# Forgetting attention: key sums subtracted inside the maximum, sample rows divided at the result

## The chip, the core and the metric

The kernel runs on one core of one Trainium2 chip. The metric is the device time of one execution in microseconds (us); the time of a kernel is the median of its timed runs. The engines of the core are TensorE (PE; its weight loads have a row of their own, PEld), VectorE (DVE), ScalarE (ACT), GpSimd (POOL) and SyncE (SP), which here mostly starts transfers. Each engine takes its instructions in the order in which they stand in its queue.

## The reference

One inference step of an encoder layer: stick-breaking attention, a Mamba-2 SSD group and forgetting attention run side by side on the same normalised input; then come an output projection, cross-attention and a feed-forward block. What the change touches is the forgetting attention ("fox"):

```python
def fox_attend(q, k, v, fq, fk, q_pos, k_pos):
    s = jnp.einsum('bqhd,bkhd->bhqk', q, k).astype(jnp.float32) * (HEAD_DIM ** -0.5)
    s = s + (jnp.transpose(fq, (0, 2, 1))[..., :, None] - jnp.transpose(fk, (0, 2, 1))[..., None, :])
    valid = k_pos[None, :] <= q_pos[:, None]
    p = jax.nn.softmax(jnp.where(valid, s, -jnp.inf), axis=-1)
    return jnp.einsum('bhqk,bkhd->bqhd', p, v.astype(jnp.float32)).astype(q.dtype)
```

fq and fk are the same running sum of log forget gates (fcum = cumsum(logf)), taken at the query and at the key. For one query, fq is one number for all keys, so in exact arithmetic it drops out of the softmax.

There are 4 fox heads of 64 columns. The prompt is one stream of 1024 tokens. The samples are 8 streams of 16 new tokens, each with 1024 cached keys and values, so a sample row has 1024 + 16 keys; the kernel lays out 128 columns for the new keys of all streams and masks.

## The kernel before, in words

**Tiling.** A row of work is 128 queries against their keys. For the prompt there are 4 heads x 8 blocks of 128 queries; block qb has (qb + 1) x 128 keys, taken in pieces of 512. For the samples there are 4 groups (two streams x 4 heads x 16 queries = 128 rows) with 1152 columns: two pieces of 512 cached keys and one of 128 new ones.

**One prompt row** (`prompt_rows`, then `fox_rows`). The key sums of the head lie in a tile "xc", loaded once per head by `fcb_of` (L732) and spread over the 128 partitions. L532, on ScalarE, writes fq - fk into a tile "ws" over the whole width of the row. Then for each piece TensorE makes the scores in a PSUM tile "pss" (L562, L563, and the mask with L565), and L536, on VectorE, adds ws to them, writes the sum back to ws and takes the running maximum into a small tile "sm". L540 negates the maximum, L542 (ScalarE) takes the exponential and its sum, L543 the reciprocal, and L549 (VectorE; the constant FSC is "D" throughout) multiplies the row by it.

**Behind two rows** (`prompt_av`) TensorE transposes the weights (L580), ScalarE copies them out (L583, tile "pt"), TensorE multiplies by the values (L595, PSUM "pso"), ScalarE (L603, L606) and VectorE (L604) take the result, and SP stores it (L608).

**One group of sample rows** (`decode_units`). The cached keys come by DMA (L883, tile "wr"), are transposed on TensorE and copied by ScalarE (L891, tile "kf"); L874 makes the scores. The key sums of the cached keys come by L910 into a tile "xc" (from fs_sc), those of the new keys lie in "fnew", and the query's own sum in "fqs"; L532 has two passes per group, over 1024 and 128 columns. Then the row goes the same way as a prompt row. In `av` the weights are transposed and copied (L926, into the tile "act"), multiplied by the new and the cached values (L934; the values come by L943), and L953 (VectorE) multiplies the result by a head mask "maskh"; L960 stores it. The stick-breaking samples run through the same `av` with m == 0.

**What runs beside it.** `pipeline` hands out rows and their products, first of the stick-breaking attention (m == 0), then of the fox (m == 1), with the sample groups inserted after units 4, 8, 12 and 16 of the latter; between two steps `fill_all` puts in a piece of the dense input projections (L328 to L330) and, when these are done, of the SSD blocks. An SSD block loads its inputs with three transfers (L1038, L1040, L1042, into a tile "act"), transposes and copies them (L1055 to L1060), makes decay weights with ScalarE (L1078, L1083) and VectorE (L1097), and ends with a norm (L1162) and a store (L1171). SP also loads the residual rows (L1282, into "st" and "xc") towards the end of the stage.

**The order.** The program is recorded in the order in which these generators emit it; then a list scheduler with a timeline of its own reorders it, engine by engine, by priority and by estimated readiness:

```python
with tile.TileContext(nc, schedule_with_timeline_sim=True) as tc:
```

So an edit in `fox_rows` also changes where other instructions stand.

**Buffers.** "ws" has 7 buffers, "xc" 3, "act" 6, "pss" 2. A transfer into a buffer waits in SP's queue until its last reader is done, and everything behind it in that queue waits too. The key sums in "xc" are last read by L532.

Of the kernel before, what the change touches and what calls it, by code (L numbers as in the profile page):

```python
# [12 lines left out]
ALU = mybir.AluOpType  # L13
# [49 lines left out]
def tile_hybrid_step(ctx: ExitStack, tc: tile.TileContext, a: dict):  # L63
# [459 lines left out]
        pool_tt(sg[:, :n - 1], sg[:, :n - 1], kp[:, 1:n], ALU.mult)  # L523
        return sg

    fcount = [0]

    def fox_rows(n, pieces, fkb, fq):
        sp = ws_t()
        mx = small(6)  # L530
        for c0, w, fk in fkb:
            ACT.activation(sp[:, c0:c0 + w], fk, AF.Identity, bias=fq, scale=-1.0)  # L532
        for i, (c0, w, emit) in enumerate(pieces):
            ps = pS()
            emit(ps[:, :w])
            DVE.tensor_tensor_reduce(out=sp[:, c0:c0 + w], in0=ps[:, :w], in1=sp[:, c0:c0 + w],  # L536
                                     op0=ALU.add, op1=ALU.max, scale=1.0,
                                     scalar=-3e38 if i == 0 else mx[:, i - 1:i], accum_out=mx[:, i:i + 1])
        np_ = len(pieces)
        DVE.tensor_scalar(mx[:, 3:4], mx[:, np_ - 1:np_], -1.0, None, ALU.mult)  # L540
        s = sp[:, :n]
        ACT.activation(s, s, AF.Exp, bias=mx[:, 3:4], accum_out=mx[:, 4:5])  # L542
        DVE.reciprocal(mx[:, 5:6], mx[:, 4:5])  # L543
        fcount[0] += 1
        e = FSC[fcount[0] % len(FSC)]
        if e == "A":
            ACT.activation(s, s, AF.Copy, scale=mx[:, 5:6])
        else:
            (DVE if e == "D" else POOL).tensor_scalar(s, s, mx[:, 5:6], None, ALU.mult)  # L549
        return sp  # L550

    def prompt_rows(m, qs, kh, kl, qb, fcb=None, fq=None):
        n = (qb + 1) * P
        mask = mask_fx if m else mask_sb
        pieces = []
        for c0 in range(0, n, 512):
            w = min(512, n - c0)

            def emit(ps, c0=c0, w=w):
                q = qs[:, qb * P:(qb + 1) * P]  # L560
                last = c0 + w == n
                PE.matmul(ps, q, kh[:, c0:c0 + w], start=True, stop=False)  # L562
                PE.matmul(ps, q, kl[:, c0:c0 + w], start=False, stop=not last)  # L563
                if last:
                    PE.matmul(ps[:, w - P:w], identr, mask, start=False, stop=True)  # L565
            pieces.append((c0, w, emit))
        if m == 0:
            return sb_rows(n, pieces)
        return fox_rows(n, pieces, [(0, n, fcb[:, :n])], fq)

    def prompt_av(h, qp, w0, w1, vt, kt_row):

# [40 lines left out]
    def prompt_units(m, h, fcb_of=None):  # L613
        env = {}

        def load():
            if not env:
                env["st"] = load_stacks(m, h)
                env["fcb"] = fcb_of(h) if m else None

        def row(qb):
            load()
            qs, kh, kl, _ = env["st"]
            return prompt_rows(m, qs, kh, kl, qb, env["fcb"], fqc[:, qb, h:h + 1] if m else None)

        def unit(qp):
            return ([lambda: row(2 * qp), lambda: row(2 * qp + 1)],
                    lambda w: prompt_av(h, qp, w[0], w[1], env["st"][3], 2 * m + h // 2))
        return [unit(qp) for qp in (range(4) if (m, h) not in REV else range(3, -1, -1))], load
# [23 lines left out]
    fqc = mcst.tile([P, 8, 4], F32, name="fqc")  # L653
    fnew = mcst.tile([P, P], F32, name="fnew")
    fqs = mcst.tile([P, 4], F32, name="fqs")

    def fox_sums():
        l = log1p_exp_negabs(lf, [P, NBLK, 4])
# [182 lines left out]
    def decode_units(m):  # L841
# [15 lines left out]
        def rows(p):  # L857
# [49 lines left out]
            if m == 0:  # L907
# [1 line left out]
            fkb = xc_t()  # L909
            SP.dma_start(out=fkb[:, :PAST],  # L910
                         in_=fs4[8 * p:8 * p + 8].rearrange("r i k -> (r i) k").unsqueeze(1).to_broadcast([32, 4, PAST]))
            return fox_rows(T, pieces, [(0, PAST, fkb[:, :PAST]), (PAST, P, fnew)], fqs[:, p:p + 1]), hold

        def av(p, w, hold):
            vsm = new[1]

            wt = hold[:, P:P + 1024] if m else st_t(F32)
            wn = hold[:, P + 1024:2 * P + 1024] if m else sg2_t()[:, :P]
            for k0 in (0, 4, 8):
                nk = min(4, 9 - k0)  # L920
                tp = pT()
                for k in range(nk):
                    wk = w[:, 8 * P:9 * P] if k0 == 8 else \
                        w[:, k0 * P:(k0 + 4) * P].rearrange("q (p k) -> q p k", k=4)[:, :, k]
                    PE.transpose(tp[:, k * P:(k + 1) * P], wk, ident)
                ACT.copy(wn if k0 == 8 else wt[:, k0 * P:(k0 + 4) * P], tp[:, :nk * P])  # L926

            po = pO()

            def quads(w, moving, start, stop):  # L930
                def one(g):
                    v = moving(g // 2, g % 2)
                    out = po[32 * g:32 * g + 32, :P]
                    return PE.matmul(out if len(v.shape) == 2 else out.rearrange("p (h d) -> p h d", h=2),  # L934
                                     w[:, 32 * g:32 * g + 32], v, start=start, stop=stop)
                return [lambda g=g: one(g) for g in (3, 0, 1, 2)]

            work = quads(wn, lambda b2, nb: vsm[:, 2 * nb:2 * nb + 2, 0, :], True, False)
            for hf in range(2):
                raws = []  # L940
                for b2 in range(2):
                    raw = ring.tile([P, 1056], F32, tag=("wh", "wl")[b2], name="vr")
                    SP.dma_start(out=raw[:, :1024].rearrange("p (k c) -> p k c", c=256),  # L943
                                 in_=cv[2 * p + b2, hf * 512:(hf + 1) * 512, :]
                                 .rearrange("(p k) c -> p k c", k=4))
                    raws.append(raw)
                for k in range(4):
                    work += quads(wt[:, (4 * hf + k) * P:(4 * hf + k + 1) * P],
                                  lambda b2, nb, raws=raws, k=k: raws[b2][:, k * 256 + nb * P:k * 256 + (nb + 1) * P],
                                  False, hf == 1 and k == 3)  # L950
            together(work)
            ob = sg2_t()[:, :P]
            DVE.tensor_tensor(out=ob.rearrange("p (h d) -> p h d", h=2),  # L953
                              in0=po[:, :P].rearrange("p (h d) -> p h d", h=2),
                              in1=maskh.unsqueeze(2).to_broadcast([P, 2, 64]), op=ALU.mult)
            of = pT()
            PE.matmul(of[:, :64], ob, fold2.rearrange("p n t -> p (n t)"), start=True, stop=True)
            on = sg2_t()[:, :64]
            DVE.tensor_copy(on, of[:, :64])
            SP.dma_start(out=mix_sc[2 * m:2 * m + 2, :, SEQ + 32 * p:SEQ + 32 * p + 32].rearrange("n p t -> p n t"),  # L960
                         in_=on.rearrange("p (n t) -> p n t", n=2))
# [1105 lines left out]
```

## Time and profile before

| what | value |
|---|---|
| median of 3 runs | 1888.05 us (1887.65 to 1890.45) |
| profiled execution, its own time | 1882.73 us |
| span of the profile | 1881.0 us |
| mean granted TensorE clock | 0.993 |
| PE busy | 1821.7 us (97%) |
| PEld busy | 1628.8 us (87%) |
| DVE busy | 892.0 us (47%) |
| ACT busy | 822.5 us (44%) |
| POOL busy | 613.0 us (33%) |

The profile shows one execution. The span runs from its first to its last instruction; some 1.7 us of the execution's time lie around it. A row such as "L532 ACT ACTIVATE ws<-xc,fqs 128x1024 x4 | 4.6, 1156" gives the line, the engine, what is written and read, the count, then the busy time in us and the mean of one in ns; behind a second bar stands the idle time of the engine just before, and what ended it. In the list of waits "PE pss L874 <- DVE sm L536: 3.6, 2, 2.7" reads: TensorE was idle for 3.6 us before L874 and VectorE's L536 ended it, in 2 waits, the longest of 2.7. SPq is SP's queue of transfers. In the busy times by stretch each column is the busy time in that stretch, and the share "DMA" is of the core's 16 DMA engines. In the chain of waits a row gives its start, its length and the work.

### The profile page before, as it was taken

The numbers are of one execution on the slowest core, as the hardware profiler recorded it, in microseconds if no ns is written. First come the engines' busy times: TensorE is split into PE (matmuls) and PEld (weight loads), VectorE is DVE, ScalarE is ACT, GpSimd is POOL, SyncE is SP. The second block draws the span as 40 slices with busy tenths as digits, with TensorE's granted clock in tenths as the row PEclk, the third lists the DMA queues.
The fourth block names the chain that finished last, engine by engine and source line by source line (L and its number), as shares of the span: only waits on it lengthen the run. The fifth ranks groups of instructions, "written<-read, shape, count | busy, mean of one in ns | idle before, by whom it ended". The sixth has DMA issues, their size and how long they took to land.

```text
span 1881.0 us, 32406 instructions
## 1 busy us (share of the span) xinstructions
PE 1821.7 (97%) x12136; PEld 1628.8 (87%) x12136; DVE 892.0 (47%) x1802; ACT 822.5 (44%) x1751; POOL 613.0 (33%) x921
## 2 busy tenths in 40 slices
PE   7999989999998989999999989999999999999998
PEld 5899878888867768899988889999999999788886
DVE  3412333566667873444443596333333334455554
ACT  6532543545567862344432464333333333344433
POOL 7622424445116653101112107444444542000000
PEclk9999998999999999999999989999999999999999
DMA  9464754437688782245585124332222223657572
GB/s 336 151 191 149 217 146 124 149 111 202 209 240 267 269 276 95 107 137 178 173 284 188 68 73 123 79 83 72 71 71 71 71 72 104 216 185 239 178 245 88
DMA packets 291069, 296.64 MB, mean 158 GB/s; under 512 B 80092, under 2 KB 242884, under 8 KB 290912
## 3 DMA queue, kind: packets, MB, share of 16 engines
q1 hardware_dynamic: 290912, 294.57, 49.9%
q8 instruction: 96, 1.57, 0.3%
q14 instruction: 61, 0.50, 0.1%
HBM read 225.12 MB, written 69.91 MB: 157 GB/s over the span
## 4 chain that ended last, share of the span: by engine, by line
PE 62%; DMA 3%; DVE 2%; ACT 2%; issue 1%; POOL 1%; SPq 0%; DVEq 0%; POOLq 0%; ACTq 0%
PE psd L1869 11%; PE pst L1869 8%; PE psd L328 5%; PE psd L329 5%; PE psd L330 5%; PE pss L1869 4%; PE pss L328 3%; PE pss L329 3%; PE pss L330 3%; PE pso L1869 2%; PE pst L328 1%; PE pst L329 1%; PE pst L330 1%; PE pso L328 1%; PE pso L330 1%
## 5 line engine op out<-in xcount | busy, mean ns | idle before, releaser
L132 POOL TENSOR_TENSOR wl<-wr,wh 128x256 fp32r<-128x256 f32 (+2 forms) x184 | 138.4, 784 | 230.8 <-ACT wh L292 220.0
L328 PE MATMUL psd<-act,wh 128*128 128x384 f32 x528 | 181.4, 344 | 0.0
L329 PE MATMUL psd<-act,wh 128*128 128x384 f32 x528 | 180.7, 342 | 0.0
L330 PE MATMUL psd<-act,wl 128*128 128x384 f32 x528 | 180.7, 343 | 0.0
L1869 PE MATMUL pst<-bT,tr 128*128 128x256 f32 (+1 forms) x1068 | 155.0, 293 | 0.0
L1869 PEld LDWEIGHTS pst<-bT,tr 128*128 128x128 f32 x1068 | 144.9, 188 | 0.1
L330 PE MATMUL psd<-wh,act 128*128 128x512 f32 (+3 forms) x424 | 136.5, 323 | 0.0
L329 PE MATMUL psd<-wl,act 128*128 128x256 f32 (+3 forms) x414 | 133.9, 324 | 1.9 <-POOL wl L132 1.9
L328 PE MATMUL psd<-wh,act 128*128 128x256 f32 (+3 forms) x414 | 132.9, 325 | 1.0 <-DMA act<-osc 0.9
L1869 PE MATMUL psd<-bT,tr 128*128 128x320 f32 (+1 forms) x912 | 133.0, 295 | 0.4 <-POOL tr L132 0.4
L1869 PEld LDWEIGHTS psd<-bT,tr 128*128 128x128 f32 x912 | 125.1, 189 | 0.7 <-POOL tr L132 0.7
L132 POOL TENSOR_TENSOR tr<-u,tr 128x256 fp32r<-128x256 f32 x110 | 82.4, 778 | 102.3 <-ACT tr L1705 84.8
L253 POOL TENSOR_SCALAR sm<-sm 128x1 f32<-128x1 f32 (+2 forms) x27 | 7.0, 260 | 301.4 <-ACT y L1971 207.2
L1844 DVE TENSOR_TENSOR tr<-tr,pst 128x256 f32<-128x256 f32 (+1 forms) x86 | 38.6, 449 | 139.9 <-ACT tr L1841 106.7
L132 POOL TENSOR_TENSOR ws<-ws 128x256 f32<-128x256 f32 (+2 forms) x100 | 69.7, 724 | 99.1 <-DVE ws L522 90.8
L330 PEld LDWEIGHTS psd<-act,wl 128*128 128x128 f32 x528 | 99.2, 188 | 2.4 <-issue 2.1
L328 PEld LDWEIGHTS psd<-act,wh 128*128 128x128 f32 x528 | 99.4, 188 | 2.0 <-issue 1.4
L329 PEld LDWEIGHTS psd<-act,wh 128*128 128x128 f32 x528 | 99.3, 188 | 1.9 <-issue 1.5
L132 POOL TENSOR_TENSOR tr<-raw,tr 128x256 fp32r<-128x256 f32 x94 | 69.8, 771 | 84.0 <-ACT tr L1705 79.2
L1705 ACT CAST tr<-tr 128x384 fp32r<-128x384 f32 (+1 forms) x70 | 37.6, 538 | 122.2 <-DMA tr<-hidsc 103.1
L292 ACT CAST wh<-wr 128x512 fp32r<-128x512 f32 (+2 forms) x90 | 52.4, 621 | 80.5 <-PE psd L330 30.6
L329 PEld LDWEIGHTS psd<-wl,act 128*128 128x128 f32 x414 | 79.2, 191 | 9.3 <-POOL wl L132 4.1
(640 smaller groups left out, 4737.0 us busy)
## 6 DMA issues: line engine op xcount, KB each, us to landing
u<-w_down SPq DMA_DIRECT2D x40, 512.0 KB
raw<-w_down SPq DMA_DIRECT2D x26, 512.0 KB
st<-qksc SPq DMA_DIRECT2D x48, 256.0 KB
wr<-w_in SPq DMA_DIRECT2D x44, 256.0 KB
tr<-hidsc SPq DMA_DIRECT2D x57, 192.0 KB
hidsc<-tr SPq DMA_DIRECT2D x34, 288.0 KB
qksc<-sg SPq DMA_DIRECT2D x48, 192.0 KB
wr<-cache_sb_k SPq DMA_DIRECT2D x32, 256.0 KB
```

Of the source, the lines that this page charges most:

```text
L132: POOL.tensor_tensor(out=out[:, a0:a1], in0=in0[:, a0:a1], in1=in1[:, a0:a1], op=op)
L253: POOL.tensor_scalar(v, ss, inv, EPS, ALU.mult, ALU.add)
L292: ACT.copy(hi, raw)
L328: PE.matmul(out, ah, bh, start=start, stop=False)
L329: PE.matmul(out, ah, bl, start=False, stop=False)
L330: PE.matmul(out, al, bh, start=False, stop=stop)
L1705: ACT.copy(hi, src)
L1844: DVE.tensor_tensor(out=at(out, g), in0=at(x, g), in1=ps[g][:, :GW[g]], op=op)
L1869: PE.matmul(dst[g][:, :GW[g]], x[:, ka], y[:, k, :], start=start and k == 0 and m == 0, stop=stop and k == 3 and m == 2, skip_group_check= ...
```

## The change

`fox_rows` no longer gets the query's sum for prompt rows. There VectorE's piece-wise operation subtracts the key sums straight from the scores and takes the maximum, reading "xc" as its second operand; ScalarE's pass L532 is not issued. Sample rows keep that pass, but are not multiplied by their reciprocal: the reciprocal goes to a new tile "frs" (one column per group), and the product with the head mask in `av` becomes a product with frs and the mask (for m == 0 with 1.0 and the mask).

```diff
--- before.py
+++ after.py
@@ -523,33 +523,31 @@
         pool_tt(sg[:, :n - 1], sg[:, :n - 1], kp[:, 1:n], ALU.mult)
         return sg
 
-    fcount = [0]
-
-    def fox_rows(n, pieces, fkb, fq):
+    def fox_rows(n, pieces, fk, fq=None, rs=None):
         sp = ws_t()
         mx = small(6)
-        for c0, w, fk in fkb:
-            ACT.activation(sp[:, c0:c0 + w], fk, AF.Identity, bias=fq, scale=-1.0)
+        if fq is not None:
+            for c0, w, src in fk:
+                ACT.activation(sp[:, c0:c0 + w], src, AF.Identity, bias=fq, scale=-1.0)
         for i, (c0, w, emit) in enumerate(pieces):
             ps = pS()
             emit(ps[:, :w])
-            DVE.tensor_tensor_reduce(out=sp[:, c0:c0 + w], in0=ps[:, :w], in1=sp[:, c0:c0 + w],
-                                     op0=ALU.add, op1=ALU.max, scale=1.0,
+            DVE.tensor_tensor_reduce(out=sp[:, c0:c0 + w], in0=ps[:, :w],
+                                     in1=fk[:, c0:c0 + w] if fq is None else sp[:, c0:c0 + w],
+                                     op0=ALU.subtract if fq is None else ALU.add, op1=ALU.max, scale=1.0,
                                      scalar=-3e38 if i == 0 else mx[:, i - 1:i], accum_out=mx[:, i:i + 1])
         np_ = len(pieces)
         DVE.tensor_scalar(mx[:, 3:4], mx[:, np_ - 1:np_], -1.0, None, ALU.mult)
         s = sp[:, :n]
         ACT.activation(s, s, AF.Exp, bias=mx[:, 3:4], accum_out=mx[:, 4:5])
+        if rs is not None:
+            DVE.reciprocal(rs, mx[:, 4:5])
+            return sp
         DVE.reciprocal(mx[:, 5:6], mx[:, 4:5])
-        fcount[0] += 1
-        e = FSC[fcount[0] % len(FSC)]
-        if e == "A":
-            ACT.activation(s, s, AF.Copy, scale=mx[:, 5:6])
-        else:
-            (DVE if e == "D" else POOL).tensor_scalar(s, s, mx[:, 5:6], None, ALU.mult)
+        DVE.tensor_scalar(s, s, mx[:, 5:6], None, ALU.mult)
         return sp
 
-    def prompt_rows(m, qs, kh, kl, qb, fcb=None, fq=None):
+    def prompt_rows(m, qs, kh, kl, qb, fcb=None):
         n = (qb + 1) * P
         mask = mask_fx if m else mask_sb
         pieces = []
@@ -566,7 +564,7 @@
             pieces.append((c0, w, emit))
         if m == 0:
             return sb_rows(n, pieces)
-        return fox_rows(n, pieces, [(0, n, fcb[:, :n])], fq)
+        return fox_rows(n, pieces, fcb)
 
     def prompt_av(h, qp, w0, w1, vt, kt_row):
 
@@ -621,7 +619,7 @@
         def row(qb):
             load()
             qs, kh, kl, _ = env["st"]
-            return prompt_rows(m, qs, kh, kl, qb, env["fcb"], fqc[:, qb, h:h + 1] if m else None)
+            return prompt_rows(m, qs, kh, kl, qb, env["fcb"])
 
         def unit(qp):
             return ([lambda: row(2 * qp), lambda: row(2 * qp + 1)],
@@ -653,6 +651,7 @@
     fqc = mcst.tile([P, 8, 4], F32, name="fqc")
     fnew = mcst.tile([P, P], F32, name="fnew")
     fqs = mcst.tile([P, 4], F32, name="fqs")
+    frs = mcst.tile([P, 4], F32, name="frs")
 
     def fox_sums():
         l = log1p_exp_negabs(lf, [P, NBLK, 4])
@@ -909,7 +908,7 @@
             fkb = xc_t()
             SP.dma_start(out=fkb[:, :PAST],
                          in_=fs4[8 * p:8 * p + 8].rearrange("r i k -> (r i) k").unsqueeze(1).to_broadcast([32, 4, PAST]))
-            return fox_rows(T, pieces, [(0, PAST, fkb[:, :PAST]), (PAST, P, fnew)], fqs[:, p:p + 1]), hold
+            return fox_rows(T, pieces, [(0, PAST, fkb[:, :PAST]), (PAST, P, fnew)], fqs[:, p:p + 1], frs[:, p:p + 1]), hold
 
         def av(p, w, hold):
             vsm = new[1]
@@ -950,9 +949,9 @@
                                   False, hf == 1 and k == 3)
             together(work)
             ob = sg2_t()[:, :P]
-            DVE.tensor_tensor(out=ob.rearrange("p (h d) -> p h d", h=2),
-                              in0=po[:, :P].rearrange("p (h d) -> p h d", h=2),
-                              in1=maskh.unsqueeze(2).to_broadcast([P, 2, 64]), op=ALU.mult)
+            DVE.scalar_tensor_tensor(ob.rearrange("p (h d) -> p h d", h=2), po[:, :P].rearrange("p (h d) -> p h d", h=2),
+                                     frs[:, p:p + 1] if m else 1.0, maskh.unsqueeze(2).to_broadcast([P, 2, 64]),
+                                     ALU.mult, ALU.mult)
             of = pT()
             PE.matmul(of[:, :64], ob, fold2.rearrange("p n t -> p (n t)"), start=True, stop=True)
             on = sg2_t()[:, :64]
```

From the first edit on the lines of the changed kernel lie two below those of before (L536 is now L535, L583 is L581, L549 is L547), and from the new tile on one below (L732 is L731, L910 is L909, L953 is L952).

The instructions of TensorE, GpSimd and SP are the same in number. ScalarE has 32 fewer, VectorE 4 fewer; 48 of the 60 piece-wise maxima read xc and subtract. The scheduler places the stage of the fox rows anew; ahead of it and behind it the order is the same but for a few rows at the start of the feed-forward block.

ScalarE, at the end of one sample group's row (the exponential over 1152 columns) while the third head begins. ws and sm are the row and its small numbers, pt the transposed weights, act the SSD block's and the samples' tiles. Before:

```order
L542 ACTIVATE ws,sm<-ws,sm 128x1152
L583 COPY pt<-pst 128x512
L532 ACTIVATE ws<-xc,fqc 128x640
L532 ACTIVATE ws<-xc,fqc 128x768
L1162 ACTIVATE act,sm<-sg 128x512
L583 COPY pt<-pst 128x384
L542 ACTIVATE ws,sm<-ws,sm 128x128
L926 COPY act<-pst 128x512 x2
```

And in the changed kernel:

```order
L542 ACTIVATE ws,sm<-ws,sm 128x1152
L581 COPY pt<-pst 128x512
L601 COPY so<-pso 64x256
L581 COPY pt<-pst 128x512 x2
L1161 ACTIVATE act,sm<-sg 128x512
L542 ACTIVATE ws,sm<-ws,sm 128x128
L925 COPY act<-pst 128x512
L581 COPY pt<-pst 128x384
```

The passes from xc into ws are gone, and copies of transposed weights stand in their place; the copies for the samples (L925) are spread between the prompt's rows.

SP, around the load of the last sample group's key sums (xc<-fs); the three loads act<-xbcsc, act<-acsc and act<-zsc belong to an SSD block. Before:

```order
L1171 DMA mixsc<-sg 128x4x128
L1040 DMA act<-acsc 128x1024
L1042 DMA act<-zsc 128x512
L910 DMA xc<-fs_204 128x1x1024
L960 DMA mixsc<-so 128x2x32
L1038 DMA act<-xbcsc 128x8x128
L1040 DMA act<-acsc 128x1024
```

And in the changed kernel, first the SSD block's loads and then, further down, the load of the sums:

```order
L1037 DMA act<-xbcsc 128x8x128
L1039 DMA act<-acsc 128x1024
L1041 DMA act<-zsc 128x512
L1037 DMA act<-xbcsc 128x8x128
L959 DMA mixsc<-so 128x2x32
```

```order
L882 DMA wr<-cache_fox_k 128x512 x3
L942 DMA vr<-cache_fox_v 128x1024 x2
L909 DMA xc<-fs_204 128x1x1024
L882 DMA wr<-cache_fox_k 128x512
L1281 DMA xc<-x_sample 128x1024
```

The load of the sums went from ahead of the SSD block's loads to behind them, among the loads of the samples' own keys and values.

SP, at the load of the third head's key sums (xc<-fcsc), in the changed kernel:

```order
L507 DMA st<-qksc 64x1024
L508 DMA st<-qksc 64x1024
L731 DMA xc<-fcsc 128x1024
L798 DMA zsc<-sg 128x256
L909 DMA xc<-fs_204 128x1x1024
L1037 DMA act<-xbcsc 128x8x128
L882 DMA wr<-cache_fox_k 128x512
```

and before:

```order
L979 DMA act<-ssd_norm_g 128x512
L732 DMA xc<-fcsc 128x1024
L608 DMA mixsc<-so 64x256
L799 DMA zsc<-sg 128x256
L883 DMA wr<-cache_fox_k 128x512
L910 DMA xc<-fs_204 128x1x1024
```

The first load of an SSD block moved up, from twelve rows behind the third head's sums to three.

## The prediction

> **What bounds the kernel now.** I read the page's engine table first, then the busy times by stretch, then who ended TensorE's idle time, then the chain of work that ended last, and last the sync engine's own waits.
>
> ```profile
> PE 1821.7 (97%) x12136; PEld 1628.8 (87%) x12136; DVE 892.0 (47%) x1802; ACT 822.5 (44%) x1751; POOL 613.0 (33%) x921
> ```
>
> Over the whole span TensorE is the bound. The forgetting attention's rows lie between 440 and 720 us, together with the SSD blocks, and there the picture is another one:
>
> ```profile
> core 0: us, PE busy (x) PEld busy (x) DVE busy (x) ACT busy (x) POOL busy (x), PEclk, DMA share, GB/s
> 440.00:520.00 80.00, 78.59 (x610) 73.08 (x609) 45.55 (x104) 42.36 (x91) 24.79 (x49) 1.00 0.71 209
> 520.00:560.00 40.00, 37.05 (x320) 25.87 (x319) 24.67 (x94) 28.53 (x63) 5.26 (x10) 1.00 0.76 227
> 560.00:600.00 40.00, 36.94 (x336) 28.44 (x333) 28.22 (x78) 29.28 (x66) 25.71 (x43) 1.00 0.80 263
> 600.00:640.00 40.00, 36.88 (x267) 27.92 (x266) 32.26 (x96) 32.04 (x72) 23.01 (x40) 1.00 0.85 290
> 640.00:680.00 40.00, 35.00 (x316) 27.48 (x315) 34.87 (x89) 32.97 (x71) 30.05 (x48) 1.00 0.86 291
> 680.00:720.00 40.00, 36.76 (x248) 29.18 (x247) 20.26 (x34) 13.53 (x24) 11.23 (x18) 1.00 0.46 153
> sum 280.00, PE 261.22 PEld 211.96 DVE 185.83 ACT 178.70 POOL 120.04; mean PE 43.54 PEld 35.33 DVE 30.97 ACT 29.78 POOL 20.01
> ```
>
> TensorE is idle for 280 - 261.2 = 18.8 us here, and that is what a better feed can win at most while its own instructions stay as they are. From 560 to 640 it idles 3.06 + 3.12 us; ScalarE is busy 73 and 80% there, VectorE 71 and 81%. Who ended the idle time, in the largest rows:
>
> ```profile
> PE pss L874 <- DVE sm L536: 3.6, 2, 2.7
> PE psd L1055 <- DVE sg L1097: 2.8, 3, 1.4
> PE psd L328 <- ACT ws L1372: 1.9, 1, 1.9
> PE pst L1130 <- ACT sg L1132: 1.8, 1, 1.8
> PE pss L562 <- DVE sm L536: 1.4, 2, 0.8
> ```
>
> VectorE ends more of it (7.8 us in three rows) than ScalarE (3.7 in two). But VectorE itself stands behind ScalarE, as the chain shows between 589 and 637 us:
>
> ```profile
> 589.37 1.18 ACT ws L532 x2
> ...
> 595.56 0.94 ACT ws L532
> ...
> 600.29 2.48 DMA act<-acsc
> 602.76 4.46 DMA xc<-fs
> ...
> 608.46 0.30 ACT ws L532
> ...
> 609.13 0.41 ACT ws L532
> ...
> 635.27 0.82 ACT ws L532 x2
> ```
>
> In these 48 us the chain passes five times through the pass that the change takes out (L532), and in between through the transfers of the SSD block (acsc) and of the samples' key sums (fs).
>
> **ScalarE loses 32 passes.** One row per query block is gone for each of four heads. The pass without the samples:
>
> ```profile
> sum 240.00, ACT 30.09; mean ACT 5.02
> L532 ACT ACTIVATE ws<-xc,fqs 128x1024 f32<-128x1024 f32 x4 | 4.6, 1156 | 0.4 <-DMA xc<-fs 0.4
> L532 ACT ACTIVATE ws<-fnew,fqs 128x128 f32<-128x128 f32 x4 | 1.6, 398 | 0.6 <-DMA fqs<-fnsc 0.6
> ```
>
> The first row is all of L532 between 440 and 680 us; 30.1 - 4.6 - 1.6 = 23.9 us leave ScalarE, a seventh of the 178.7 us that it works in the stage. On the path lie only the pieces of the chain: 1.18 + 0.94 = 2.12 us before 600, and 0.30 + 0.41 + 0.82 = 1.53 us after it. The rest runs beside TensorE; before 520 TensorE idles 1.4 us in 80, so passes there win nothing.
>
> **The sync queue.** The key sums (xc) were last read by L532; now the head's last maximum on VectorE reads them. SP waits in its queue for that reader before it can load the next sums:
>
> ```profile
> SPq L732 <- ACT ws L532: 5.7, 1, 5.7
> SPq L910 <- ACT pt L583: 1.7, 1, 1.7
> 602.76 0.55 SPq L910 DMA_DIRECT2D xc<-fs  x1
> ...
> 604.80 0.50 SPq L1038 DMA_DIRECT2D act<-xbcsc  x1
> ```
>
> The second stop holds the SSD block's load (L1038) behind the last sample's sums. In the new order that load of the sums stands 16 printed rows further back, behind the SSD loads, so the stop of 1.7 us leaves this place; the chain's pieces at 600 and 602 us are exactly these transfers. I take 1.4 us, between nothing (the transfers share the same engines anyway) and the 4.46 us of the chain's piece. What gets later is the release, and it costs something if SP is early:
>
> ```profile
> 556.80 1.17 ACT L532 ACTIVATE ws<-xc,fqc 128x1024 f32<-128x1024 f32 x1
> 562.55 0.74 DVE L536 CUSTOM_DVE_ANT_0 ws<-pss,ws,sm 128x512 f32<-128x512 f32 x1
> 564.53 4.54 SPq L883 DMA_DIRECT2D wr<-cache_fox_k  x3
> ```
>
> For the second head the last pass ended at 557.97, the last maximum at 563.29: 5.3 us more. Behind it on SP stand a store, a state store and the next keys (L883), which were issued at 564.53 in any case, 1.2 us after. So I cost the later release at zero here; without that cover it is 5.3 us (below).
>
> **VectorE.** Four normalising passes over the sample rows go, eight mask products become products with a scalar, and the maximum reads another SBUF tile and subtracts:
>
> ```profile
> L549 DVE TENSOR_SCALAR ws<-ws,sm 128x1152 f32<-128x1152 f32 x4 | 3.6, 897 | 0.0
> L953 DVE TENSOR_TENSOR so<-pso,maskh 128x128 f32<-128x128 f32 x5 | 1.4, 286 | 1.5 <-PE pso L934 1.4
> L1145 DVE SCALAR_TENSOR_TENSOR act<-act,psd 128x128 f32<-128x128 f32 x16 | 4.9, 341 | 3.7 <-PE pst L1140 3.0 <-PE psd L1140 0.6
> L536 DVE CUSTOM_DVE_ANT_0 ws<-pss,ws 128x512 f32<-128x512 f32 x24 | 16.3, 679 | 6.2 <-PE pss L563 2.7 <-PE pss L874 2.5 <-ACT ws L542 1.0
> L536 DVE CUSTOM_DVE_ANT_0 ws<-pss,ws,sm 128x512 f32<-128x512 f32 x8 | 6.0, 744 | 4.5 <-PE pss L565 3.6 <-PE pss L874 0.8
> ```
>
> That is 4 x 0.897 = 3.6 us less, and 8 x (341 - 286) ns = 0.4 us more. The subtracting maximum has no row. Its shape, sources and sink are those of L536; I take 679 ns, between the same and the 744 ns of the form that also reads a scalar, which would add 32 x 65 ns = 2.1 us. A gain in it has no source: width and PSUM operand stay. One of the four passes lies between 600 and 640 us, where VectorE is 81% busy and ends TensorE's waits; I count it with 0.8 us and the other three with zero, since they stand beside TensorE's own work in stretches where it is 92% busy or where no chain row of VectorE is. Four reciprocals only change their target.
>
> By the Trainium skill (Perfetto Trace Analysis, Identifying the Most-Contended Engine) improving a kernel means improving its most-contended engine. That would be VectorE from 640 on, with 34.9 of 40 us, and the sum by that rule would be little more than the 0.8 us; the chain rows of L532 speak against it before 640.
>
> **The sum.** In 560 to 600: 2.12 us of the 3.06 idle. In 600 to 640: 1.53 + 1.4 + 0.8 = 3.73, more than TensorE's idle time of 3.12, so 3.12. After 640 the chain has no L532, and I take nothing of the 5.0 us. Together 5.2 us. The profiled execution took 1882.73 us with a span of 1881.0; it would take 1877.5. The median of the runs, 1888.05, lies 5.3 above that execution, and the same saving gives 1882.8. The forecast's own range is 2.1 us (only the first stretch holds) to 6.2 us (both stretches' idle time): 1881.9 to 1885.9.
>
> **Rivals.** *The stage is bound by latency, and gains more.* TensorE's loads are busy for only 27.5 to 28.4 of 40 us from 560 to 680, so its "busy" 92% may hold short matmuls that wait for one another. Then every pass taken out of ScalarE's queue there pulls the whole row of work forward: L532's 15.2 us from 560 to 680, less 3 x 1.55 for the samples, is 10.5 us, and 1877.5. For it: ScalarE's back-to-back stretches. Against: the same TensorE column. The three rows of that price:
>
> ```profile
> 560.00:600.00 40.00, 5.04 (x7) 1.00 0.80 263
> 600.00:640.00 40.00, 6.51 (x9) 1.00 0.85 290
> 640.00:680.00 40.00, 3.63 (x4) 1.00 0.86 291
> ```
>
> The Trainium skill, on the same page and section, calls matmul busy time a poor measure and asks for the weight loads' share instead; by it the headroom would be 12 us in 40, and this rival the likelier one.
>
> *Nothing measurable.* VectorE ends TensorE's waits, the next chain lies a few hundred ns under ScalarE's, and only VectorE's 0.8 us arrive: 1887.2. For it: 7.8 us against 3.7 in the waits. Against: the chain.
>
> *Slower: SP stands behind the held sums.* The release is 5.3 us later, and SP is in order. If the last maximum of a head comes more than the 1.2 us of slack after SP gets there, the next keys and the SSD block's loads are late; the third head's sums now stand three rows ahead of the first SSD load, where twelve lay between. The chain holds such a key load:
>
> ```profile
> 571.65 8.04 DMA wr<-cache_fox_k
> ```
>
> One such stop in full costs 5.3 us, 1893.3. For it: three of the later loads now wait for VectorE by the names of their readers. Against: the rows' maxima themselves come earlier when they no longer wait for ScalarE.
>
> That the passes stay is excluded: they are not in ScalarE's new order.
>
> **Numbers.** The forecast gets 0.42, latency 0.20, nothing 0.20, slower 0.18. A change under 0.2% (3.8 us) can't be told from none here. Faster: the forecast's part above 3.8 us of gain, 0.32, and latency, 0.20: 0.52. Same: 0.10 and 0.18 of the rest: 0.28. Slower: 0.18 and 0.02 for an unlucky order among the same instructions: 0.20. The range runs from 1874 (latency with another 3.5 us of the 18.8) to 1891 (more than half of a full SP stop), and leaves out some 0.05 below and 0.12 above.
>
> **What would show it.** In the changed profile L532's line has eight instructions and ScalarE is busy some 24 us less; its share of the chain between 589 and 637 us shrinks; the stop of SP before the last sample's sums no longer stands ahead of an SSD load; VectorE is some 3 us less busy and the maximum still takes 0.68 us; TensorE's idle time from 440 to 720 falls from 18.8 to about 14 us, and before 440 nothing moves. I am wrong if TensorE's idle time stays (then VectorE was the feed), if it falls by 8 us or more (latency), or if SP waits for the maximum for several us.

## The result, and the profile after

Over 22 runs of each, the changed kernel took 1885.81 us (median; 1880.35 to 1894.55) and the kernel before 1890.03 us (1882.71 to 1900.08). The medians differ by 4.2 us. The ratio on record, which is not the quotient of the two medians, is 0.9969 (95% interval 0.9956 to 0.9982): 5.9 us faster, where 5.2 us were forecast. In a second set of runs, on another chip, the ratio was 0.998 (0.9965 to 0.9995), 3.8 us, and the medians differ by 3.2 us. Faster is settled; whether by 3 or by 6 us is not. Two executions of the experiments below, one of 1968.75 us at a granted clock of 0.874 and one of 9651.18 us, lie far outside all others and are left out of the ratios.

The first profile of the changed kernel has a span of 1892.8 us and the one of before 1881.0 us, which says the opposite of the 22 runs. Two single executions can't be set against each other here, so both kernels were profiled a second time:

```profile
core 0: 1888.1 us, clock 0.992
core 0: 1894.0 us, clock 0.990
```

The first row is the changed kernel, the second the one before. The stage of the attention rows is now read in one window from 440 to 740 us, at whose ends TensorE is hardly idle. The busy times by stretch, in this order: the kernel before, before again, the change, the change again (columns: us, then busy time and instructions of PE, PEld, DVE, ACT, POOL, then the granted clock, the DMA share, GB/s):

```profile
core 0: us, PE busy (x) PEld busy (x) DVE busy (x) ACT busy (x) POOL busy (x), PEclk, DMA share, GB/s
440.00:740.00 300.00, 281.22 (x2170) 228.24 (x2169) 191.57 (x499) 183.11 (x392) 125.38 (x214) 1.00 0.71 226
440.00:740.00 300.00, 279.07 (x2141) 226.38 (x2140) 191.14 (x494) 182.76 (x392) 129.68 (x215) 0.98 0.73 228
440.00:740.00 300.00, 286.61 (x2150) 229.66 (x2149) 186.37 (x493) 162.88 (x360) 132.46 (x215) 0.97 0.71 229
440.00:740.00 300.00, 286.84 (x2171) 232.13 (x2170) 190.17 (x496) 163.43 (x362) 133.39 (x215) 0.98 0.72 230
```

TensorE is idle for 300 minus the first column: 18.8 and 20.9 us before, 13.4 and 13.2 us after. In these two pairs the number repeats within some 2 us between executions of one program, and it fell by 5 to 8 us. ScalarE works about 20 us less. The granted clock of the stage was 1.00 in the first profile of before and 0.97 to 0.98 in the other three: the first one was lucky.

The engine table of the change, and the operation that no row of before had (first profile of the change by line and shape):

```profile
PE 1837.7 (97%) x12136; PEld 1638.6 (87%) x12136; DVE 886.4 (47%) x1798; ACT 802.1 (42%) x1719; POOL 617.9 (33%) x921
L535 DVE CUSTOM_DVE_ANT_0 ws<-pss,xc 128x512 f32<-128x512 f32 x20 | 13.6, 679 | 2.7 <-PE pst L578 1.7 <-PE pss L561 1.1
```

The subtracting maximum takes 679 ns, the value taken. Who ended TensorE's idle time in the stage, before (second profile) and with the change (second profile):

```profile
PE pss L874 <- DVE sm L536: 3.6, 2, 2.7
PE psd L1055 <- DVE sg L1097: 2.8, 3, 1.4
PE psd L1133 <- DVE act L1072: 2.6, 1, 2.6
PE pst L1130 <- ACT sg L1132: 2.4, 1, 2.4
...
PE pss L562 <- DVE sm L536: 1.5, 1, 1.5
```

```profile
PE psd L1094 <- ACT sg L1169: 2.0, 1, 2.0
PE psd L1054 <- DMA act<-xbcsc: 1.8, 2, 1.4
PE pst L888 <- DMA wr<-cache_fox_k: 1.6, 1, 1.6
PE pso L933 <- ACT act L925: 1.5, 1, 1.5
PE psd L1168 <- DVE st L1321: 1.3, 1, 1.3
```

The waits for the maximum (L536, now L535), 5.1 us in two rows, are gone from the head of the list. Read by itself this is the forecast come true: the pass is gone, so the maximum comes sooner. The chain of work that ended last seems to agree: between 589 and 637 us it holds none of the prompt's passes any more in either profile of the change, only 1.06 us of a sample row's in the first. But the second profile of before shows how little one such chain is worth. Its pieces of the pass in the same part of the program (the same stretch some 9 us later) are

```profile
598.86 1.18 ACT ws L532 x2
...
605.05 0.94 ACT ws L532
...
643.63 0.82 ACT ws L532 x2
```

The first, second and last piece of the prediction's list are there again, the two at 608 and 609 us are not, and neither are the load of the samples' key sums (4.46 us) and the key load (8.04 us). The experiments say more.

### The profile page after: what moved, and what is told of

Read it like the earlier page. It is cut to its first block, busy times and chain, and to the rows that moved or that the text cites. A ratio compares the mean times of both kernels' runs of the same rounds, so it can differ in the third digit from the quotient of the medians.

```text
span 1892.8 us, 32368 instructions
## 1 busy us (share of the span) xinstructions
PE 1837.7 (97%) x12136; PEld 1638.6 (87%) x12136; DVE 886.4 (47%) x1798; ACT 802.1 (42%) x1719; POOL 617.9 (33%) x921
## 4 chain that ended last, share of the span: by engine, by line
PE 83%; DMA 5%; DVE 4%; POOL 3%; ACT 3%; issue 2%; SPq 0%; DVEq 0%; POOLq 0%; ACTq 0%
PE psd L1868 11%; PE psd L328 10%; PE psd L329 10%; PE psd L330 10%; PE pst L1868 8%; PE pss L1868 4%; PE pss L328 3%; PE pss L330 3%; PE pss L329 3%; PE pso L1868 2%; POOL wl L132 2%; PE pst L328 1%; PE pst L329 1%; PE pst L330 1%; PE pso L593 1%
```

## The experiments

Each is given as a ratio to the kernel before, timed beside it on the same chip. They ran in three groups, each on one chip: the change again, its halves and the pass kept in the chain; then the pass kept aside, the two shifted kernels and the one with no pass at all; last the held orders and the kernel before again.

### The change again, and its two halves

The second run of the change is the one above.

> The whole change again, for a second profile and more times. My theory (ScalarE's pass on the path): 5.9 us under before as in the first runs (0.9969), and in the stage of the fox rows TensorE idles some 5 us less than the 18.8 us of before. Rival (the times differ by the throttle alone): the ratio comes out at 1.000 and the stage's idle time is as before.

It came to 0.998 (0.9965 to 0.9995), 1887.77 us, with 13.2 us of idle TensorE in the window. "The throttle alone" (the granted clock, and nothing else) falls for the idle time; the distance in time is between the two.

The subtraction alone takes the division out of the change again:

```diff
-            return fox_rows(T, pieces, [...], fqs[:, p:p + 1], frs[:, p:p + 1]), hold
+            return fox_rows(T, pieces, [...], fqs[:, p:p + 1]), hold
...
-                                     frs[:, p:p + 1] if m else 1.0, maskh...
+                                     1.0, maskh...
```

> Only the subtraction inside the maximum; the sample rows are normalised on VectorE as before, and the product with the mask takes 1.0. My theory: nearly all of the gain, 4.4 to 5.1 us under before (0.9973 to 0.9977), since the terms of ScalarE and of the sync queue are here and only VectorE's 0.8 us is not. Rival (VectorE was the feed, so that the four passes of 0.9 us did it): 0 to 2 us under before. Rival (the gain is the luck of the scheduler's new order): anything from 4 us above to 8 us under.

The division alone gives the prompt rows their pass and their query sums back:

```diff
-        return fox_rows(n, pieces, fcb)
+        return fox_rows(n, pieces, [(0, n, fcb[:, :n])], fqc[:, qb, h:h + 1])
```

> Only the sample rows' division moved to the result; the prompt rows keep ScalarE's pass and the addition. My theory: 0 to 1 us under before (0.9995 to 1.0). Rival (VectorE is the feed): 3 us or more under before. Rival (order): anything.

The subtraction alone was 1.0013 (1.0 to 1.0026), the division alone 1.0026 (1.0009 to 1.0043): 1892.17 and 1896.26 us. No half gains, one loses, and the whole gains. Costs that add up can't do this. Their rows of the window:

```profile
440.00:740.00 300.00, 283.53 (x2156) 230.10 (x2156) 194.30 (x499) 161.60 (x358) 132.62 (x214) 0.98 0.71 228
440.00:740.00 300.00, 284.00 (x2135) 229.55 (x2134) 187.50 (x489) 183.43 (x395) 130.96 (x216) 0.95 0.72 227
```

The subtraction alone has ScalarE's work as low as the whole change (161.6 us) and 16.5 us of idle TensorE, 3 us more than the change. The division alone has ScalarE's work as it was (183.4 us), and TensorE idles 16.0 us, 3 to 5 us less than before, although the kernel is slower: the stage's idle time doesn't tell the time of the whole. My theory wanted nearly all of the gain in the subtraction; it got none in time. And the waits for the maximum, which had seemed to hang on the pass, by the waits of the subtraction alone and of the division alone:

```profile
PE pss L873 <- DVE sm L535: 0.6, 1, 0.6
PE pss L873 <- DVE sm L535: 3.6, 2, 2.7
```

The second is the kernel before's own row (3.6 us, 2 waits, the longest 2.7). So where the pass stays the waits stay, and where it goes they go. That fits the theory as well as it fits another order of VectorE's queue, and the last group of runs decides between the two. What it shows here already: the waits went in the subtraction alone, its chain between 500 and 740 us holds no piece of the pass either, and it gained no time.

### The pass kept, in the chain and aside

```diff
+        if fq is None:
+            ACT.activation(sp[:, :n], fk[:, :n], AF.Identity, bias=fqc[:, 0, 0:1], scale=-1.0)
```

> The whole change, but for each prompt row ScalarE still makes a pass of the same width from the key sums into the row's tile ahead of the maximum, which then overwrites it: the pass stands in the row's chain and on ScalarE as before, and nobody reads it. My theory: 4 us or more of the gain is gone, 0 to 2 us under before (0.999 to 1.0). Rival (the gain comes from VectorE or from the later reader of the key sums): as the whole change, 5 to 6 us under before. Rival (order): anything.

1.0032 (1.0016 to 1.0047), 1896.10 us: slower than before, not equal to it. Aside, into the unused columns of the row's tile:

```diff
+        if fq is None:
+            dead = sp[:, n:].bitcast(mybir.dt.bfloat16)
+            room = 2 * (T - n)
+            for c0 in range(0, n, room):
+                w = min(room, n - c0)
+                ACT.activation(dead[:, :w], fk[:, c0:c0 + w], AF.Identity, bias=fqc[:, 0, 0:1], scale=-1.0)
```

> The whole change, with ScalarE still making its pass over the key sums for every prompt row, but into the unused end of the row's tile (as bf16, in 2 and 4 parts for the two widest rows), so that no instruction waits for it: ScalarE is as busy as before, and the row's chain is as short as in the change. If what counted was ScalarE's time (its queue being in order): most of the gain is gone, 0 to 2 us under before (0.999 to 1.0). If what counted was the pass in the row's chain: as the whole change, 4 to 6 us under before (0.997 to 0.998), with 12 to 13 us of idle TensorE in the stage.

1.0035 (1.0019 to 1.0050), 1900.46 us, with this row of the window:

```profile
440.00:740.00 300.00, 281.59 (x2133) 225.25 (x2133) 188.50 (x491) 187.32 (x411) 131.97 (x215) 0.97 0.72 227
```

Both lost all of the gain and more. Taken for themselves the two would support the theory that the pass's time is on the path; but both overshoot the kernel before, whose ScalarE does nearly the same work (183 us against 187 here; the parts of the widest rows cost something).

### The same work in another order

Each of these edits gives the scheduler another program, and it makes another order. How much is that worth alone? One constant was changed, in the kernel before and in the changed one; the instructions are the same in number and kind, and their order differs from the SSD blocks on:

```diff
-    acc = 0.0
+    acc = 0.5
```

> The kernel before with the same work recorded half a step otherwise: the counter that decides when a piece of the filling work (projections, SSD blocks) is put between two attention rows starts at 0.5, so that the scheduler makes another order from the SSD blocks on. My theory (the passes set the time of the stage): within 2 us of before (0.999 to 1.001). Rival (the scheduler's luck decides at this scale): 3 us or more from before, on either side.

> The whole change with the same half step. My theory: it stands 3 to 6 us under the shifted kernel before, as the change stood under before, and TensorE's idle time in the stage is again some 6 us less. Rival (order): the distance between the two shifted kernels is anything, 0 or the other way too.

The kernel before went to 1.0042 (1.0020 to 1.0064), 1902.09 us, and the change to 1.0038 (1.0023 to 1.0052), 1902.31 us. Another order alone costs the kernel before 8 us, more than the whole change brings, and in this order the change brings nothing that the runs can tell. The two rows of the window (before shifted, change shifted):

```profile
440.00:740.00 300.00, 278.08 (x2090) 220.29 (x2089) 186.80 (x492) 179.78 (x386) 127.72 (x208) 0.95 0.69 220
440.00:740.00 300.00, 278.43 (x2130) 226.08 (x2130) 191.43 (x491) 164.36 (x366) 134.11 (x213) 0.97 0.71 226
```

TensorE idles 21.9 and 21.6 us, although ScalarE works 15 us less in the second. In the shifted change TensorE waits most for the loads of the samples' cached keys:

```profile
PE pst L888 <- DMA wr<-cache_fox_k: 8.5, 5, 2.5
```

In the two profiles of before these waits are 1.4 and 0.6 us. And the shifted kernel before is 8 us slower with only 1 to 3 us more idle time in the window, another sign that this idle time isn't all that counts. What the rest is stays open.

One more kernel took the pass away from the sample rows too:

```diff
-            for c0, w, src in fk:
-                ACT.activation(sp[:, c0:c0 + w], src, AF.Identity, bias=fq, scale=-1.0)
...
-                                     op0=ALU.subtract if fq is None else ALU.add, op1=ALU.max, scale=1.0,
+                                     op0=ALU.subtract, op1=ALU.max, scale=1.0,
```

> The whole change, and the sample rows too subtract their key sums inside the maximum: ScalarE makes none of these passes, 8 fewer (6.2 us). My theory: another 0 to 2 us, 0.996 to 0.998 of before, since two pieces of the chain at 589 and 595 us may have been the samples' passes. Rival (VectorE and the sync queue feed the stage now): the same as the whole change within 1 us. Rival (order): anything.

1.0000 (0.9982 to 1.0018), 1894.98 us: the kernel with the least work on ScalarE (155.4 us in the window) shows no gain.

```profile
440.00:740.00 300.00, 281.32 (x2137) 227.25 (x2136) 188.38 (x491) 155.38 (x349) 131.16 (x213) 0.97 0.72 229
```

### The order held, the work taken out

So the order has to stay while the work goes. In three programs every instruction was left where the scheduler had put it, with its waits, and only then were the 32 prompt passes cut to one column. In the two kernels with the old maximum, before and before shifted, the maxima read that one column, so that the prompt's forgetting terms are left out; in the third nobody reads what the passes write. In the traces of all three pairs the instructions of every engine stand in the same order. The edit in the kernel before:

```diff
+            o = int(len(fkb) == 1)
-            ACT.activation(sp[:, c0:c0 + w], fk, AF.Identity, bias=fq, scale=-1.0)
+            ACT.activation(sp[:, c0 + o:c0 + w + o], fk, AF.Identity, bias=fq, scale=-1.0)
...
-                                     in1=sp[:, c0:c0 + w],
+                                     in1=sp[:, c0:c0 + w] if len(fkb) > 1 else sp[:, n:n + 1].to_broadcast([P, w]),
...
+    ins[n] = mybir.InstActivation(func=i.func, name=i.name, engine=i.engine, debug=i.debug,
+                                  ins=[last_column(x) for x in i.ins], outs=[last_column(x) for x in i.outs],
+                                  sync_info=i.sync_info)
```

> The kernel before in its own order on every engine, every instruction and every wait in its place, but each of the 32 prompt passes of ScalarE works on one column instead of 128 to 1024 (the maxima add that column to all scores, so the prompt's forgetting terms are left out). This takes ScalarE's time out and leaves the order as it was. My theory (the pass's time is on the path): 3 to 6 us under before (0.997 to 0.9985), TensorE's idle time in the stage falls from 18.8 to 13 to 15 us. Rival (the scheduler's new order made the gain of the change): within 1 us of before, idle time 18 us or more.

> The same in the order of the shifted kernel before (which took 1902.1 us, 1.0042 of before): its 32 prompt passes work on one column. My theory: 3 to 6 us under the shifted kernel, 1.001 to 1.0026 of before. Rival (order): as the shifted kernel, 1.0042.

> The kernel that kept the pass in the row's chain beside the whole change (1896.1 us, 1.0032), in its own order, with the 32 passes on one column; here no result is left out, since nobody reads what they write. My theory: 3 to 6 us under that kernel, 1.0 to 1.0016 of before. Rival (order): as it was, 1.0032.

> The kernel before against itself, for a second profile: ratio 1.000 within its interval. If the first profile was typical, TensorE again idles 18 to 19 us in the stage; if the first profile was a lucky one, the stretch ahead of the stage takes some 454 us instead of 450 and the throttle is seen in the stage.

The passes of one column, from the first of the three by line and shape:

```profile
L533 ACT ACTIVATE ws<-xc,fqc 128x1 f32<-128x1 f32 x32 | 8.8, 295 | 5.2 <-PE pst L581 5.2
```

They still take 8.8 us of the 23.9, so 15 us are out and not all. What it brought:

| order | with the pass | pass on one column |
|---|---|---|
| of before | 1.0014 (0.9992 to 1.0035) | 0.9991 (0.9970 to 1.0013) |
| of before, shifted | 1.0042 (1.0020 to 1.0064) | 1.0035 (1.0012 to 1.0058) |
| of the pass kept in the chain | 1.0032 (1.0016 to 1.0047) | 1.0032 (1.0013 to 1.0052) |

The first cell is the kernel before against itself. The steps are 2.3, 0.7 and 0.0 thousandths, and none is clear of the intervals. Where the first is counted from 1.000, which is what the kernel before has by definition, it is 0.9. The idle time of TensorE, which moved by 5 to 8 us with the change, moves less here:

```profile
440.00:740.00 300.00, 281.09 (x2132) 227.69 (x2131) 189.27 (x493) 167.61 (x391) 129.90 (x215) 0.96 0.72 226
440.00:740.00 300.00, 280.38 (x2116) 223.53 (x2115) 186.57 (x492) 165.85 (x386) 130.98 (x212) 0.97 0.70 224
440.00:740.00 300.00, 280.09 (x2134) 225.97 (x2133) 189.34 (x489) 168.56 (x391) 131.30 (x215) 0.97 0.72 227
```

18.9 us in the order of before (18.8 and 20.9 with the pass), 19.6 in the shifted one (21.9), 19.9 in the last (22.0 with the pass, from the row below). So 15 us less on ScalarE bring between 0 and 2.3 us of idle time; if all 23.9 went at the same rate, 0 to 3.7 (an estimate).

```profile
440.00:740.00 300.00, 278.04 (x2136) 224.95 (x2135) 189.26 (x490) 182.84 (x389) 128.81 (x213) 0.98 0.72 228
```

And the waits for the maximum, the 5 us that the change removed, do not move. Who ended TensorE's idle time with the pass on one column, in the order of before:

```profile
PE pss L875 <- DVE sm L537: 3.6, 2, 2.7
...
PE pss L563 <- DVE sm L537: 1.2, 1, 1.2
```

They are 3.6 and 1.2 us, where 3.6 and 1.5 stood with the passes. In the order of the pass kept in the chain the two rows are 2.2 and 1.1 us with the pass, 2.1 and 1.3 without. The wait of 2.7 us, the largest of the stage, is there with the pass and without it. VectorE's timeline tells why; the kernel before, ahead of that wait's end, and TensorE's row:

```profile
664.41 0.56 DVE L255 SCALAR_TENSOR_TENSOR sm<-sm 128x1 f32<-128x1 f32 x1 [0.42 <-POOL sm L254]
665.00 0.65 DVE L256 TENSOR_TENSOR sm<-sm 128x1 f32<-128x1 f32 x1
665.58 1.35 DVE L1373 TENSOR_TENSOR ws<-ws 128x1152 fp32r<-128x1152 f32 x1
666.85 0.67 DVE L257 SCALAR_TENSOR_TENSOR sm<-sm 128x1 f32<-128x1 f32 x1
667.45 0.68 DVE L536 CUSTOM_DVE_ANT_0 ws<-pss,ws 128x512 f32<-128x512 f32 x1
...
668.28 1.06 PE L874 MATMUL pss<-kf,act 128*32 128x512 f32 x8 [2.70 <-DVE sm L536]
```

And with the passes on one column:

```profile
676.17 0.56 DVE L255 SCALAR_TENSOR_TENSOR sm<-sm 128x1 f32<-128x1 f32 x1 [0.42 <-POOL sm L254]
676.76 0.65 DVE L256 TENSOR_TENSOR sm<-sm 128x1 f32<-128x1 f32 x1
677.34 1.35 DVE L1374 TENSOR_TENSOR ws<-ws 128x1152 fp32r<-128x1152 f32 x1
678.61 0.67 DVE L257 SCALAR_TENSOR_TENSOR sm<-sm 128x1 f32<-128x1 f32 x1
679.21 0.68 DVE L537 CUSTOM_DVE_ANT_0 ws<-pss,ws 128x512 f32<-128x512 f32 x1
...
680.03 1.62 PE L875 MATMUL pss<-kf,act 128*32 128x512 f32 x8 [2.70 <-DVE sm L537]
```

The maximum was not waiting for ScalarE. It stood in VectorE's queue behind three small steps of an SSD norm (L255 to L257), the first of which waited 0.42 us for GpSimd (L254), and behind L1373, 1.35 us that split an output projection's input, work of the next stage. In the changed kernel the scheduler put this split behind the last sample rows. Its second profile:

```profile
680.60 0.69 DVE L535 CUSTOM_DVE_ANT_0 ws<-pss,ws 128x512 f32<-128x512 f32 x1
...
682.48 0.74 DVE L535 CUSTOM_DVE_ANT_0 ws<-pss,ws,sm 128x512 f32<-128x512 f32 x1
...
687.02 1.92 DVE L1372 TENSOR_TENSOR ws<-ws 128x1152 fp32r<-128x1152 f32 x1
```

The two halves agree with this reading: with the division alone the same four instructions stand ahead of the maximum and the wait is 2.70 us; with the subtraction alone the split stands behind the last sample row, as in the change.

That is one wait of 2.7 us followed to its place in the queue. A program in which only the split is moved was not run. The other waits that went (some 3 us net) were not followed one by one, and the reverse test, the order of the change with the pass put back, wasn't made: both kernels that put the pass back came out in other orders.

## Why the prediction was right, and where it was wrong

**The time** was forecast 5.2 us lower and came 5.9 and 3.8 us lower by the ratios (4.2 and 3.2 us by the medians), inside the forecast's own range of 2.1 to 6.2 us in both sets. TensorE's idle time from 440 to 720 us was to fall to about 14 us; it fell to 13.4 and 13.2.

**The bound** was right in part. The stage is where the change acts, and its idle time fell as forecast. But the time of the whole doesn't follow that idle time alone, as the prediction took it to: the division alone idles 3 to 5 us less there and is slower, and the shifted kernel before idles 1 to 3 us more and is 8 us slower.

**The first term of the sum was wrong**: "In 560 to 600: 2.12 us of the 3.06 idle", and with it the 1.53 us after 600. It took the pieces of the pass in the chain as time that is won when they go. With the order held, 15 of the pass's 23.9 us brought between 0 and 2.3 us of idle time in three orders, and the time itself moved by less than its intervals. So the pieces were worth something between nothing and, for all of the pass, some 3.7 us, but the waits for the maximum that ended when the change came in were not theirs. The chain itself was one execution's: in the second profile of before it held 2.94 us of the pass instead of 3.65.

**The waits were misread.** The prediction said that "VectorE itself stands behind ScalarE". For the largest wait this is refuted: VectorE was working on other things, and it was the order of its own queue that made TensorE wait. For the smaller ones it is open.

**The missing rival.** Both kernels do what they do in an order that a scheduler makes anew after each edit, and the prediction gave that 0.02 ("an unlucky order among the same instructions"). The order turned out to be worth more than the change: half a step in one constant cost 8 us, two halves of the change were not faster than before, and their sum was. The gain of 3 to 6 us is real for these two programs. The waits for the maximum, 5.1 us before and 0.7 us after, are 4.4 of the 7.8 us by which the idle time fell from one second profile to the other. They went with the new order: they stay when the passes shrink and the order is held. What the passes' time brings beside it is 0 to 3.7 us by the idle time, and can't be told closer.

**Luck.** That the number came out is in good part luck. Three other kernels without the prompt's passes, the subtraction alone, the shifted change and the one with no pass at all, came to 1.0013, 1.0038 and 1.0000; nothing in the prediction makes any of them slower than the change by more than 0.8 us.

**The other terms.** The sync queue's 1.4 us can't be told apart from the order, of which that move was a part, and the chain's piece behind it (4.46 us) isn't in the second profile of before. The later release of the key sums was costed at zero, and the rival in which it stops SP did not come: the largest waits of SP's queue for these loads in the second profile of the change are

```profile
SPq L731 <- ACT ws L531: 1.2, 1, 1.2
SPq L909 <- DMA act<-ssd_norm_g: 0.9, 1, 0.9
```

and no row of these loads is for a maximum. In the first profile L731 stood 4.1 us, for ScalarE as well; before, 5.7 and 4.5 us stood for L732. VectorE's price was right in both terms that could be read: 679 ns for the new maximum, and for the product with frs (second profile of the change)

```profile
L952 DVE SCALAR_TENSOR_TENSOR so<-pso,frs,maskh 128x128 f32<-128x128 f32 x4 | 1.4, 347 | 3.7 <-PE pso L933 3.6
```

347 ns against 341 taken. Over the whole span VectorE is 4 to 7 us less busy, where some 3 were forecast, and ScalarE 20 to 21, where some 24 were: the sum of the passes, 23.9 us, counts twice the 0.1 us by which a pass can overlap the next instruction (one from 502.32 lasts 1.15 us, the next starts at 503.38). Whether VectorE's removed passes bring the 0.8 us wasn't measured; the division alone made the kernel slower, in an order that kept the wait of 2.7 us.

**The rival of latency** asked for a fall of the idle time by 8 us or more. From 440 to 720 us it fell by 5.4 and 5.6 us from the first profile of before, by 7.5 and 7.8 from the second, and the time by 3 to 6 us: it didn't come. Its price was also mis-summed: two groups of sample rows have their passes between 560 and 680 us (at 603 and 648 us), not three, so that 15.2 - 2 x 1.55 gives 12.1 us and not 10.5.

## What to carry to other kernels

Where a scheduler writes the order, an edit is two edits, and for a change of a few tenths of a per cent the second may be the larger: run the same work in another order first, to learn what the order alone is worth. To price the work itself, hold the order and shrink the instruction in place; a wait that stays to the hundredth of a microsecond was not the instruction's. A wait "for VectorE" is read in VectorE's timeline just ahead of it: what it worked on tells whether it was late or only badly queued.

## What the runs showed of the hardware

The time of one execution goes with the clock that TensorE is granted. In 241 runs of the kernel before and of these experiments, each set taken against its own mean, time and granted clock lie on a line of 1.36 us per 0.001 of mean clock (correlation -0.86), and single runs of the kernel before lie between 0.982 and 0.994. Set to a clock of 0.990 by that line, the means differ a little from one set and chip to the next: the kernel before comes to 1891.3, 1893.1 and 1892.0 us on three chips, and to 1894.2 in its own second set on the last of them. So only kernels of one chip are set against each other. On the first of these chips the change has 1889.1 us, 2.2 less than the kernel before; the subtraction alone 1892.7 and the division alone 1893.9, still slower. On the second the two shifted kernels have 1899.1 and 1900.9 us, 6.0 and 7.8 more: the order's effect stays. The change's gain is smaller at an equal clock than as run, because it also had the better mean clock (0.9908, against 0.9896 for the kernel before beside it); for its first 22 runs (0.9916) the clock of the kernel before is not on record. Why a program is granted more, and whether its order has a part in it, stays open: the kernel with the division alone had 0.9877 on the same chip.

With this spread, one profile of each kernel compared by its span told of a loss of 12 us (1892.8 against 1881.0) where 22 runs of each show a gain of 4 to 6.
